# Channel shuffle on one core: the head's small tiles are merged, and the 38 KB tiles walk the array in pairs

## The chip, the core and the metric

The kernel runs on one core of a Trainium2 chip. The core has a vector engine (DVE), a scalar engine (ACT), a GpSimd engine (POOL), a sync engine (SP) and a tensor engine (PE). It has 128 partitions of on-chip memory (SBUF), and 16 DMA engines that move data between SBUF and the device memory (HBM). The time is device microseconds (us) of one execution; smaller is better.

## The reference

```python
# x: (16, 64, 64, 256) float32, groups = 8
channels_per_group = c // groups            # 32
x = x.reshape(batch, h, w, groups, channels_per_group)
x = x.transpose(0, 1, 2, 4, 3)
x = x.reshape(batch, h, w, c)
```

Each of the 65,536 pixels has 256 channels, which is 1 KB. Inside a pixel, an 8 x 32 matrix of channels is transposed to 32 x 8. No arithmetic is done and no value leaves its pixel. 67.11 MB are read and 67.11 MB are written.

## The kernel before

Input and output are seen as flat arrays of pixels. A *tile* is a stretch of pixels that is laid over the 128 partitions, q pixels to a partition; since a pixel has 1 KB, q is also the number of KB that each partition holds. The list `_SLOTS` (line 12) says how the 512 pixels of each partition are cut up:

- slot 0 has two pieces, 4 KB and 8 KB a partition, which share one input buffer and one output buffer;
- slot 1 has one piece of 28 KB;
- slots 2 to 13 have one piece of 38 KB each;
- slot 14 has one piece of 16 KB.

The loop at line 45 runs over the slots. `rows` (line 39) cuts a contiguous stretch of P * q pixels out of the flat array and gives each partition q of them in a row, so that the pixels of partition p + 1 begin where those of partition p end. A piece takes three steps:

- **Load**, line 55: `nc.sync.dma_start`, issued by SP. On the DMA side these are the packets of queue q1.
- **Copy**, line 57: `nc.vector.tensor_copy` on DVE, which reads the channels as (group, channel in group) and writes them as (channel in group, group), from the input buffer into the output buffer.
- **Store**, line 61: `nc.scalar.dma_start`, issued by ACT. These are the packets of queue q10.

Both DMAs of a piece move 128 rows, one for each partition, and a row is contiguous in HBM and in SBUF. In the trace each row is one packet: 16 loads of 128 rows are 2,048 packets, and 16 semaphore packets of 4 bytes for each load make up the other 256 of the 2,304 that the page counts for q1. A DMA engine handles 8 of the 128 rows.

There are two input buffers and three output buffers (lines 13 and 14), each as large as the biggest slot. So the load of slot n has to wait until the copies of slot n - 2 have read that input buffer, and the copies of slot n have to wait until the stores of slot n - 3 have left that output buffer. Within an engine the order is that of the program (`manual_schedule`, line 43). SP issues nothing but loads, ACT nothing but stores, DVE nothing but copies; POOL and PE take no part.

Of the kernel before, what the change touches and what calls it, by code (L numbers as in the profile page):

```python
# [1 line left out]

# [4 lines left out]


F32 = mybir.dt.float32
P = 128  # L10

_SLOTS = [[4, 8], [28]] + [[38]] * 12 + [[16]]
_IN_BUFS = 2
_OUT_BUFS = 3


@with_exitstack
def kernel(
    ctx: ExitStack,
    tc: tile.TileContext,  # L20
    x: bass.AP,
    groups: bass.AP,
    out: bass.AP,
):
    nc = tc.nc
    b, h, w, c = x.shape
    G = int(groups)
    CPG = c // G
    assert G * CPG == c
    assert sum(map(sum, _SLOTS)) * P == b * h * w  # L30
    biggest = max(map(sum, _SLOTS))

    x_flat = x.rearrange("b h w c -> (b h w c)")
    out_flat = out.rearrange("b h w c -> (b h w c)")

    in_pool = ctx.enter_context(tc.tile_pool(name="in_pool", bufs=_IN_BUFS))
    out_pool = ctx.enter_context(tc.tile_pool(name="out_pool", bufs=_OUT_BUFS))

    def rows(flat, first, q):

        return flat[first * c : (first + P * q) * c].rearrange("(p f) -> p f", p=P)

    ctx.enter_context(tc.manual_schedule(engines=None))
    first = 0
    for parts in _SLOTS:
        in_tile = in_pool.tile([P, biggest * c], F32, name="in_tile")
        out_tile = out_pool.tile([P, biggest * c], F32, name="out_tile")
        at = 0
        pieces = []
        for q in parts:  # L50
            pieces.append((q, first, slice(at * c, (at + q) * c)))
            first += P * q
            at += q
        for q, start, cols in pieces:
            nc.sync.dma_start(out=in_tile[:, cols], in_=rows(x_flat, start, q))  # L55
        for q, start, cols in pieces:
            nc.vector.tensor_copy(  # L57
                out=out_tile[:, cols].rearrange("p (i j g) -> p i j g", j=CPG, g=G),
                in_=in_tile[:, cols].rearrange("p (i g j) -> p i j g", g=G, j=CPG),
            )  # L60
            nc.scalar.dma_start(
                out=rows(out_flat, start, q), in_=out_tile[:, cols]
            )


# [1 line left out]
_INS = ['x', 'groups']  # L67
_OUTS = [((16, 64, 64, 256), 'float32')]

_NUMBERS = {'groups': 8}  # L70


# [26 lines left out]
```

## Time and profile before

| what | value |
|---|---|
| time, median of 3 runs | 316.12 us (316.09 to 316.13) |
| span of the profiled execution | 314.4 us (314.44 from the first instruction to the last) |
| DVE busy | 119.0 us in 16 copies, 38% of the span |
| one copy of a 38 KB tile | 8.79 us (mean of 12) |
| HBM | 67.11 MB read, 67.11 MB written, 427 GB/s over the span |
| load of a 38 KB tile, issue to landing | 37.0 us (median of 12) |
| store of a 38 KB tile, issue to landing | 42.6 us (median of 12) |

The time of the runs is 1.7 us more than the span: what lies outside the first and the last instruction is counted in the one and not in the other. The issue-to-landing times are longer than a transfer takes, since a DMA is issued while the one before it on its queue is still running. The share of a DMA queue on the page is the time that its packets took, as a share of 16 engines over the whole span.

### The profile page before, as it was taken

What the parts mean: (1) busy time and instruction counts of PE and PEld (TensorE: products, weight loads), DVE (VectorE), ACT (ScalarE), POOL (GpSimd) and SP (SyncE); (2) the same over time, 40 slices, a digit from 0 to 9 for tenths busy, and PEclk for the clock granted to TensorE, in tenths of its full rate; (3) what the DMA queues carried; (4) which work ended last, traced back from release to release, by engine and by line L of the source; (5) the groups of instructions that cost most, each with busy time, mean ns of one, the idle gap of its engine ahead of it and who ended that gap; (6) DMA issues with size and microseconds to landing.
All of it is one profiled execution on the core that took longest, in us unless ns stands there. A gap on an engine that the chain in (4) does not pass through costs nothing.

```text
span 314.4 us, 132 instructions
## 1 busy us (share of the span) xinstructions
DVE 119.0 (38%) x16; POOL 0.2 (0%) x4
## 2 busy tenths in 40 slices
DVE  2081907309109109019028028037046055065400
POOL 0000000000000000000000000000000000000000
DMA  7999999999999999999999999999999999999997
GB/s 317 405 441 416 435 416 483 401 465 406 450 421 446 426 436 436 401 470 396 475 396 475 396 470 401 470 401 470 401 450 421 446 426 436 436 417 450 429 421 321
DMA packets 4608, 134.22 MB, mean 427 GB/s; under 512 B 512, under 2 KB 512, under 8 KB 768
## 3 DMA queue, kind: packets, MB, share of 16 engines
q1 hardware_dynamic: 2304, 67.11, 49.8%
q10 hardware_dynamic: 2304, 67.11, 49.4%
HBM read 67.11 MB, written 67.11 MB: 427 GB/s over the span
## 4 chain that ended last, share of the span: by engine, by line
DMA 76%; DVE 19%; issue 0%; SPq 0%; DVEq 0%
DMA in_tile<-in_x_dram 76%; DVE out_tile L57 19%; SPq L55 0%; DVEq L57 0%
## 5 line engine op out<-in xcount | busy, mean ns | idle before, releaser
L57 DVE COPY out_tile<-in_tile 128x9728 f32<-128x9728 f32 (+4 forms) x16 | 119.0, 7440 | 179.4 <-DMA in_tile<-in_x_dram 179.4
L80 POOL MEMSET const-uint8-127<- 128x1 uint8 x1 | 0.1, 103 | 0.0
L80 POOL MEMSET const-bfloat16-1.0<- 128x1 bf16 x1 | 0.1, 102 | 0.0
L80 POOL MEMSET const-float32-1.0<- 128x1 f32 x1 | 0.1, 100 | 0.0
L80 POOL MEMSET const-float32-0.0<- 128x1 f32 x1 | 0.1, 99 | 0.2 <-issue 0.2
## 6 DMA issues: line engine op xcount, KB each, us to landing
in_tile<-in_x_dram SPq DMA_DIRECT2D x12, 4864.0 KB, 37.0
out_dram<-out_tile ACTq DMA_DIRECT2D x12, 4864.0 KB, 42.6
in_tile<-in_x_dram SPq DMA_DIRECT2D x1, 3584.0 KB, 14.7
out_dram<-out_tile ACTq DMA_DIRECT2D x1, 3584.0 KB, 30.9
in_tile<-in_x_dram SPq DMA_DIRECT2D x1, 2048.0 KB, 30.4
out_dram<-out_tile ACTq DMA_DIRECT2D x1, 2048.0 KB, 15.2
in_tile<-in_x_dram SPq DMA_DIRECT2D x1, 1024.0 KB, 5.4
out_dram<-out_tile ACTq DMA_DIRECT2D x1, 1024.0 KB, 25.0
```

The lines of the kernel that those rows point to most:

```text
L57: nc.vector.tensor_copy(out=out_tile[:, cols].rearrange("p (i j g) -> p i j g", j=CPG, g=G), in_=in_tile[:, cols].rearrange("p (i g j) -> ...
L80: nc = _bacc.Bacc("TRN2", target_bir_lowering=False, num_devices=1)
```

## The change

The list of slots becomes thirteen tiles of 38 KB and one of 18 KB. The pieces of 4, 8 and 28 KB at the head are gone, and so is the 16 KB piece at the end. The first 38 KB tile is taken with `rows` as before. The next twelve are taken in six pairs by a new function, `pair_half`: a pair is a contiguous stretch of 2 * P * 38 pixels in which each partition owns 76 in a row. The first tile of the pair takes the first 38 of each partition's 76, the second tile the last 38. So a row is still 38 KB and contiguous, but in HBM the rows of neighbouring partitions now begin 76 KB apart instead of 38 KB. The output is addressed in the same way. The last tile, 18 KB a partition, uses `rows`.

```diff
-_SLOTS = [[4, 8], [28]] + [[38]] * 12 + [[16]]
+_SLOTS = [[38]] * 13 + [[18]]

+    def pair_half(flat, first, q, half):
+        pair = flat[first * c : (first + 2 * P * q) * c].rearrange("(p f) -> p f", p=P)
+        return pair[:, half * q * c : (half + 1) * q * c]
...
+    paired = 0
...
         for q in parts:
-            pieces.append((q, first, slice(at * c, (at + q) * c)))
+            cols = slice(at * c, (at + q) * c)
+            if q == biggest and first:
+                half = paired % 2
+                start = first - half * P * q
+                source = pair_half(x_flat, start, q, half)
+                target = pair_half(out_flat, start, q, half)
+                paired += 1
+            else:
+                source = rows(x_flat, first, q)
+                target = rows(out_flat, first, q)
+            pieces.append((q, source, target, cols))
             first += P * q
             at += q
-        for q, start, cols in pieces:
-            nc.sync.dma_start(out=in_tile[:, cols], in_=rows(x_flat, start, q))
-        for q, start, cols in pieces:
+        for q, source, target, cols in pieces:
+            nc.sync.dma_start(out=in_tile[:, cols], in_=source)
+        for q, source, target, cols in pieces:
             nc.vector.tensor_copy(
...
-            nc.scalar.dma_start(
-                out=rows(out_flat, start, q), in_=out_tile[:, cols]
-            )
+            nc.scalar.dma_start(out=target, in_=out_tile[:, cols])
```

Buffers, engines and the order of the three steps stay: SP issues 14 loads instead of 16, DVE runs 14 copies instead of 16, ACT issues 14 stores instead of 16.

## The prediction

> **What bounds the kernel now.** I read the page's engine and DMA-queue parts first, then the chain of waits, then the table of stretches with each stretch's DMA rate.
>
> ```profile
> DVE 119.0 (38%) x16; POOL 0.2 (0%) x4
> ...
> q1 hardware_dynamic: 2304, 67.11, 49.8%
> q10 hardware_dynamic: 2304, 67.11, 49.4%
> ...
> DMA in_tile<-in_x_dram 76%; DVE out_tile L57 19%; SPq L55 0%; DVEq L57 0%
> ```
>
> DVE works 38% of the span. The two DMA queues together fill 99.2% of all 16 engines' time. The chain's 19% for DVE must not be read as "a faster copy gains 19%": the chain goes load, copy, next load into the freed buffer, and while the copy runs the engines work through the other buffer's load and the stores. That is to be seen in the second view, whose columns are the stretch, its length, DVE, POOL, clock, DMA share and GB/s:
>
> ```profile
> 1.75:9.11 7.36, 3.11 (x2) 0.00 (x0) 1.00 1.00 400
> 9.11:34.60 25.49, 10.99 (x2) 0.00 (x0) 1.00 1.00 420
> 34.60:117.35 82.75, 30.73 (x4) 0.00 (x0) 1.00 1.01 436
> 117.35:278.19 160.84, 61.61 (x7) 0.00 (x0) 1.00 1.00 434
> ...
> 294.54:313.28 18.74, 3.87 (x1) 0.00 (x0) 1.00 0.95 411
> 313.28:314.44 1.16, 0.00 (x0) 0.00 (x0) 1.00 0.00 0
> ```
>
> I cut it where the records of DMA packets change character. At 1.75 us the first packet starts, at 9.11 the first store packet, at 34.60 the first packet of the 28 KB store; from 294.54 only stores are left, and 313.28 is the end of the last packet. From 34.60 on the rate is flat at 434 to 436 GB/s. Only the head (400, then 420) and the very end (411) are below. So the bound is the rate of the DMA engines, and everything the change can win or lose without disturbing that rate lies in the first 35 us.
>
> What sets 434? In the packet records a 4 KB row takes 159 ns and a 38 KB row (38,912 bytes) 1,439 ns, in nearly all of the 3,072 cases. The slope is (1439 - 159) / (38912 - 4096) = 0.0368 ns a byte, that is 27.2 GB/s an engine, and about 8 ns a row do not depend on size. Seven tile periods of the steady part (the copies that start at 117.35 and 278.19) last 160.84 us, 22.98 each, or 1,436 ns for each of an engine's 16 rows. Bytes alone are 38912 x 0.03676 = 1,430.6 ns, so a row costs 5.5 ns beside its bytes (successive packets overlap by 3 ns in the records). That is all there is to save in the steady part: 0.4%.
>
> **The change part by part.** The reckoning is done for one engine, which moves 8.39 MB in both directions together: 8388608 x 0.03676 ns = 308.4 us. Before, it has 16 x 8 x 2 = 256 rows; 256 x 5.5 ns = 1.4; together 309.8. The trace has 313.28 - 1.75 = 311.5 from the first packet to the last, so 1.7 us are lost. The packet records say where, as a mean over the engines:
>
> - 0.22 us: the engines start their first row up to 0.56 us apart;
> - 0.29: the 4 KB load's rows take longer than 159 ns, nearly all of it the first row of each engine;
> - 0.05 and 0.26: the rows of the 8 KB and 28 KB loads (32 ns, 3%, on each 28 KB row);
> - 0.18: the first 38 KB load, at 16 to 29 us (22 ns, 1.5%, a row);
> - 0.36: one single row of the second 38 KB load, at 32.9 us, which takes about 1.81 us instead of 1.44 on all 16 engines at once;
> - the rest, some 0.3, is that the engines do not all end together.
>
> The first five, the single row included, sum to 1.36. The table of stretches gives the same: (1 - 400/434) x 7.36 + (1 - 420/434) x 25.49 = 0.57 + 0.82 = 1.39. All these slow rows are loads in a stretch where loads run almost alone; in the steady part, where loads and stores alternate, load rows of the same size are not slow, nor are the store rows at the end.
>
> *Two loads, two copies and two stores fewer.* 32 rows an engine go, 32 x 5.5 ns = -0.18 us. The page shows 5.4 us from issue to landing for the 8 KB load and 3.3 for the 4 KB load, but the later ones queue behind the earlier ones, and the engines' records have no gap between them: rows of the 8 KB load start at 3.43 us, before the last row of the 4 KB load has ended at 3.67. The copies on DVE become 13 x 8.79 + 3.87 x 18/16 = 118.6 us against 119.0, worth nothing, because each lies beside a load and a store. The issues on SP and ACT (0.33 and 0.36 us each) lie beside transfers too. [...]
>
> *The first stores are issued later.* Before, the first store is issued at 5.19 us. Now the first load must land whole: 1.75 + 0.2 + 0.3 + 8 x 1.46 = 13.9, plus 0.5 from the last packet's end to DVE's start (0.33 to 0.68 for the four loads at the head), plus the copy's 8.79: 23.2 us, at which the first store and the third load are issued. The engines are not idle meanwhile, for the second load is queued behind the first. It lasts until 13.9 + 11.7 = 25.6. What changes is that rows 2 to 16 of every engine are loads running alone. At 22 ns a row (the first 38 KB load) that is 0.33 us, at 3% of 1,439 (the 28 KB row) 0.65; I take 0.5. First-row delay and stagger, 0.29 + 0.22, stay. The single slow row of 0.36 may have belonged to the old handover from small stores to large ones, or not: bounds 0 and 0.36, value 0.18. The head's loss is then 0.22 + 0.29 + 0.5 + 0.18 = 1.19 against 1.36: -0.17. Bounds: 0.84 to 1.52, that is -0.52 to +0.16.
>
> *The cover of the first copy.* From the first load's landing the second gives the engines 11.7 us of work. Waiting, copy and the way from issue to the first packet (0.73 to 1.75, thus 1.02) take 0.5 + 8.79 + 1.02 = 10.3. 1.4 us are left, so I price it at nothing; beyond 1.4 every microsecond costs one. Behind the third load, SP has only loads that need the next copies, so it delays nothing else.
>
> *The pairs.* Rows stay 38 KB, 8 to an engine, and the packet count is the same. Only the distance between rows in HBM doubles, to 76 KB. The trace has distances of 4, 8, 16, 28 and 38 KB, none with gaps between rows. For stores all five cost the same 0.0368 ns a byte beside their 8 ns; for loads that alternate with stores so does 38. On the gain side nothing can come in the steady part beyond 5.5 ns a row (13 x 16 = 208 such rows an engine, 1.1 us), and a row still needs its packet. On the loss side the nearest row is the 3% of loads running alone: on the second tile alone, 0.35 us more. I take 0, since neither distance nor size has moved a row's time so far. [...]
>
> *The end.* The last load brings 18 KB instead of 16, and its copy takes 4.36 us instead of 3.87. Covered: after the last load lands, 18.7 us of stores are still to go. Last packet to end of span stays 1.16 us.
>
> Sum: -0.18 - 0.17 = -0.35 us on a span of 314.44: 314.1. The runs' median lies 1.68 above the span, so 315.8 us (-0.11%).
>
> **The rivals.** I count 0.2%, about what a measurement of this kernel can tell from no change, as the border: 315.49 to 316.75 is no change.
>
> *Faster.* The single slow row goes (-0.36), lone loads lose only 22 ns a row (0.33, against the 0.49 that the old 8, 28 and first 38 KB loads lost: -0.16) and 32 rows fewer give -0.18: 316.12 - 0.70 = 315.4. For it: the slow row came just before a new store's first packet. Against it: the 28 KB rows lost 3%, which is the purer case of lone loads. If the pairs help the second load too, 315.1. 24%.
>
> *Slower by a gap at the head.* The old first store was issued at 5.19 us, yet its first packet started at 9.12, 3.9 us later. If the third load needs as long as this one instead of 1.02, the cover of 1.4 is gone: 3.9 - 1.02 - 1.4 = 1.5 us idle, and 315.8 + 1.5 = 317.3. It decides from 1.0 us idle. Against it: those 3.9 us were spent behind load rows in flight, with the engines busy. 14%.
>
> *Slower by the distance of 76 KB.* Each 1% on the rows of twelve tiles is 12 x 0.23 = 2.8 us, so 1% gives 318.6; it decides from 0.4% (6 ns a row). Against it: between stores, load rows show no loss at all. 10%.
>
> *No effect of the pairing at all* is part of the forecast.
>
> **How the numbers follow.** The forecast, no change, has 52%, its own range 315.5 to 316.5. The time is its 315.8. The range 315.1 to 317.3 takes in the faster case and the head's gap, and leaves out the distance case and a few per cent of extremes. Faster 0.24, same 0.52, slower 0.14 + 0.10 = 0.24.
>
> **What would show it.** Right: 14 copies; first store issued near 23 us; no stretch of the head in which the 16 engines stand idle between 23 and 28 us; 434 GB/s in the steady part and 22.98 us from one copy to the next; q1's share still a little above q10's; q10 silent until about 25 us and stores alone for some 20 us at the end. Wrong: a tile period above 23.1 us (the distance), a hole near 26 us (the cover), or a head whose lone loads run below 420 GB/s.

## The result and the profile after

The changed kernel takes 330.74 us (median of 4 runs, 330.02 to 332.63) against 316.12: 1.047 times as long, 95% interval 1.0426 to 1.0514. The forecast was no change, at 315.8 us. The profiled execution is the run of 332.63 us, with a span of 330.9 against 314.4: 16.5 us more.

The DMA queues of the page after (packets, MB, share of 16 engines' span):

```profile
q10 hardware_dynamic: 2016, 67.11, 50.5%
q1 hardware_dynamic: 2016, 67.11, 47.6%
```

The order of the two lines has turned round. Before, the stores (q10) took 49.4% of 314.4 = 155.3 us of each engine, now 50.5% of 330.9 = 167.1: 11.8 us more for the same bytes. The loads (q1) went from 156.6 to 157.5. The stores have become slow, not the loads.

The table of stretches after, with the same columns as before:

```profile
1.74:25.30 23.56, 8.86 (x1) 0.00 (x0) 1.00 1.00 420
25.30:29.00 3.70, 2.37 (x1) 0.00 (x0) 1.00 1.02 263
...
52.77:272.09 219.32, 79.52 (x9) 0.00 (x0) 1.00 1.00 413
...
324.00:329.53 5.53, 0.00 (x0) 0.00 (x0) 1.00 0.43 183
```

Three things are to be seen. From 25.3 to 29.0 us the rate falls to 263 GB/s: a hole where the third load begins, (1 - 263/434) x 3.7 = 1.5 us. In the long middle the rate is 413 instead of 434 although the engines are busy all the time (DMA share 1.00). At the end most engines have nothing left to do (share 0.43).

The copies show the same middle as a longer period (timeline after):

```profile
15.12 8.86 DVE L72 COPY out_tile<-in_tile 128x9728 f32<-128x9728 f32 x1 [15.12 <-DMA in_tile<-in_x_dram]
24.01 11.85 ACTq L76 DMA_DIRECT2D out_dram<-out_tile  x2
26.63 8.84 DVE L72 COPY out_tile<-in_tile 128x9728 f32<-128x9728 f32 x1 [2.65 <-DMA in_tile<-in_x_dram]
52.77 8.85 DVE L72 COPY out_tile<-in_tile 128x9728 f32<-128x9728 f32 x1 [17.30 <-DMA in_tile<-in_x_dram]
...
272.09 8.84 DVE L72 COPY out_tile<-in_tile 128x9728 f32<-128x9728 f32 x1 [15.27 <-DMA in_tile<-in_x_dram]
```

From 52.77 to 272.09 lie nine periods of 24.37 us, 1.39 us more for each tile than the 22.98 of the kernel before, whose seven periods lie between these two copies (timeline before):

```profile
117.35 8.76 DVE L57 COPY out_tile<-in_tile 128x9728 f32<-128x9728 f32 x1 [14.25 <-DMA in_tile<-in_x_dram]
278.19 8.73 DVE L57 COPY out_tile<-in_tile 128x9728 f32<-128x9728 f32 x1 [14.21 <-DMA in_tile<-in_x_dram]
```

The packet records say which packets these are. A 38 KB load row still takes 1,439 ns. A 38 KB store row takes 1,583 ns in the middle (mean from 52.77 to 272.09 us), 10% more, and 1,439 again at the end, once the last loads have landed. Over an engine's 13 x 8 store rows that is 11.9 us. The rest: the loads' slow first rows cost 2.4 us where the slow rows before had cost 1.1, and the engines idle for 3.8 us on average instead of 0.6. Of these 3.2 us more, 2.6 are at the end, where one engine finishes at 329.5 us and the others between 324 and 327. 11.9 + 1.3 + 3.2 = 16.4 of the 16.5 us.

So two questions stood: which part of the change makes store rows slow, the distance of 76 KB or the new head; and by what.

### The profile page after: what moved, and what is told of

Read it like the earlier page. It is cut to its first block, busy times and chain, and to the rows that moved or that the text cites. A ratio compares the mean times of both kernels' runs of the same rounds, so it can differ in the third digit from the quotient of the medians.

```text
span 330.9 us, 121 instructions
## 1 busy us (share of the span) xinstructions
DVE 119.4 (36%) x14; POOL 0.2 (0%) x4
## 3 DMA queue, kind: packets, MB, share of 16 engines
q10 hardware_dynamic: 2016, 67.11, 50.5%
## 4 chain that ended last, share of the span: by engine, by line
DMA 78%; DVE 17%; issue 0%; SPq 0%; DVEq 0%
DMA in_tile<-in_x_dram 78%; DVE out_tile L72 17%; SPq L70 0%; DVEq L72 0%
## 5 line engine op out<-in xcount | busy, mean ns | idle before, releaser
L72 DVE COPY out_tile<-in_tile 128x9728 f32<-128x9728 f32 (+1 forms) x14 | 119.4, 8528 | 198.0 <-DMA in_tile<-in_x_dram 198.0
```

Of the source, the lines that this page charges most:

```text
L72: nc.vector.tensor_copy(out=out_tile[:, cols].rearrange("p (i j g) -> p i j g", j=CPG, g=G), in_=in_tile[:, cols].rearrange("p (i g j) -> ...
```

## The experiments

### Which part: the head or the pairs

Four kernels, each with one part.

```diff
 # head_only: after, without the pairs
-                source = pair_half(x_flat, start, q, half)
-                target = pair_half(out_flat, start, q, half)
+                source = rows(x_flat, first, q)
+                target = rows(out_flat, first, q)
 # pairs_old_head: after, with the old list of tiles
-_SLOTS = [[38]] * 13 + [[18]]
+_SLOTS = [[4, 8], [28]] + [[38]] * 12 + [[16]]
 # pair_loads: as pairs_old_head, stores contiguous
+                target = rows(out_flat, first, q)
 # pair_stores: as pairs_old_head, loads contiguous
+                source = rows(x_flat, first, q)
```

> Only the new list of tiles, thirteen of 38 KB and one of 18 KB, all with contiguous rows 38 KB apart; no pairs. Theory D (distance: rows 76 KB apart make store rows slow beside loads): the store rows go back to 1,439 ns, the tile period to 22.98 us, and only the gap near 26 us that the changed kernel shows (about 2 us) is left: 317 to 319 us. Theory H (head: the new head sets the engines in step in another way, and that makes the store rows slow): store rows stay near 1,583 ns, period near 24.3, about 330 us.

> The old list of tiles (4, 8, 28 KB, twelve of 38, 16 KB), with the twelve 38 KB tiles in pairs for loads and stores. Theory D: store rows near 1,580 ns while loads run beside them, period near 24.3 us, 326 to 331 us in all. Theory H: as before the change, 316 us, period 22.98.

> The old list of tiles; the loads of the twelve 38 KB tiles go in pairs (rows 76 KB apart), the stores keep rows 38 KB apart, so the output's pixels stand in another order; same bytes. Theory D, if what counts is where the stores write: 316 us, store rows 1,439 ns. If what counts is how load rows and store rows lie to each other, or where the loads read: between 320 and 330 us. Theory H: 316 us.

> The old list of tiles; the stores of the twelve 38 KB tiles go in pairs (rows 76 KB apart), the loads keep rows 38 KB apart, so the output's pixels stand in another order; same bytes. Theory D, if what counts is where the stores write: 326 to 331 us, store rows near 1,580 ns. If the loads' distance is needed too, less or nothing: 316 to 322 us. Theory H: 316 us.

| kernel | median us | ratio to before, 95% |
|---|---|---|
| head_only | 331.29 | 1.048 (1.044 to 1.053) |
| pairs_old_head | 316.21 | 0.999 (0.997 to 1.002) |
| pair_loads | 316.18 | 1.000 (0.999 to 1.001) |
| pair_stores | 316.15 | 1.000 (0.999 to 1.001) |

The queue lines of head_only's page are those of the changed kernel to 0.1%:

```profile
q10 hardware_dynamic: 2016, 67.11, 50.6%
q1 hardware_dynamic: 2016, 67.11, 47.6%
```

Theory D has fallen: pairs_old_head should have been slow, and pair_stores too if the stores' distance alone mattered. The distance of 76 KB cost nothing here, on either side (316.15 to 316.21 us). All of the loss comes from the list of tiles.

### How the head does it: the lead of the loads over the stores

Packet records carry no engine number, but in the steady part a packet starts within 4 ns of the end of the one before it, so most engines can be followed through. Nearly all 16 engines move in step: a round of load rows, a round of store rows, and so on. In the kernel before, all 16 end their rows of a load within about 0.5 us, in the changed kernel 14 of them within about 0.8. Number the load rows of an engine through from the first 38 KB tile (8 a tile) and the store rows in the same way, and call the difference between a store row and the load row just ahead of it the *lead*. In the kernel before it is 18 for six rows and 17 for two rows of each tile. In the changed kernel and in head_only it is exactly 16, two tiles, on nearly all engines that could be followed: the third load and the first store are issued together at 24.0 us, the moment the first copy is done. The second load is then nearly through (its last rows end between 25.4 and 26.3 us) and no store is ahead, so the two start almost level, load row first. The store row behind load row r of one tile is then row r of the tile two before. The two queues also change transfers at the same moment.

Two kernels move the lead by a hair and little else. The extra row or rows go into a buffer that nobody reads.

```diff
 # nudge_new: head_only, plus
+        if slot == 0:
+            extra = extra_pool.tile([P, 1 * c], F32, name="extra")
+            nc.scalar.dma_start(out=extra[:32, :], in_=rows(x_flat, 0, 1)[:32, :])
 # nudge_old: before, plus
+        if slot == 4:
+            extra = extra_pool.tile([P, 1 * c], F32, name="extra")
+            nc.sync.dma_start(out=extra[:16, :], in_=rows(x_flat, 0, 1)[:16, :])
```

> The new list of tiles with contiguous rows, and between the first and the second store ACT issues one extra load of 32 rows of 1 KB into a buffer that nothing reads: two short rows for each engine, 0.1 us of packets, which let the loads get ahead of the stores by two or three rows more. In the slow kernel's records the loads stand exactly 16 rows (two tiles) ahead of the stores on an engine, and store rows take 1,580 ns; in the kernel before they stand 17 and 18 rows ahead, and store rows take 1,439. Theory O (order: the exact 16 is what makes the store rows slow): store rows 1,439 ns, period 22.98, 317 to 320 us with the gap at 26 us still there. Theory G (the gap near 26 us and the 3 us first rows after it throw the engines out of step, and that makes them slow): the gap is not touched, so 330 us.

> The kernel before, and behind the third 38 KB load SP issues one extra load of 16 rows of 1 KB into a buffer that nothing reads: one short row for each engine, so that the loads lose one row, or two with the change of transfers, of their lead over the stores. No gap at the head. Theory O: where the lead becomes 16 rows, store rows become slow, and the time goes to between 318 and 328 us; if the lead goes to another number than 16 it tells nothing. Theory G: 316.3 us.

Both came out as theory O has it: at a lead of 16 the store rows became slow (1,611 and 1,589 ns in nudge_old from the third on), at leads of 17 to 19 they did not (1,439). nudge_new, with 32 KB more to move than head_only, takes 319.92 us instead of 331.29 (1.012 times before, 1.009 to 1.016). nudge_old, with 16 KB more than the kernel before and its head untouched, takes 326.49 instead of 316.15 (1.033, 1.031 to 1.034). Here are nudge_old's rounds from the packet records; each line is one round of 16 engines, and the extra row is not counted in the lead:

```
start us  queue  row of tile   mean ns   lead
   66.17  store  tile 3 row 4     1439     18
   67.60  load   tile 5 row 7     1439
   69.04  store  tile 3 row 5     1439     18
   70.48  store  tile 3 row 6     1439     17
   71.91  load   the extra row      46
   71.96  store  tile 3 row 7     1439     17
   73.40  load   tile 6 row 0     1439
   74.84  store  tile 4 row 0     1439     16
   76.27  load   tile 6 row 1     1439
   77.71  store  tile 4 row 1     1489     16
   79.17  load   tile 6 row 2     1439
   80.60  store  tile 4 row 2     1611     16
   82.28  load   tile 6 row 3     1439
   83.71  store  tile 4 row 3     1589     16
```

Until 71.9 us this is the kernel before. One short row takes a place on the load queue, the lead becomes 16, and within three rows the stores are slow. They stay so until the loads run out. nudge_old's timeline shows the period change with it:

```profile
49.01 8.92 DVE L58 COPY out_tile<-in_tile 128x9728 f32<-128x9728 f32 x1 [10.17 <-DMA in_tile<-in_x_dram]
71.19 8.81 DVE L58 COPY out_tile<-in_tile 128x9728 f32<-128x9728 f32 x1 [13.26 <-DMA in_tile<-in_x_dram]
98.28 8.72 DVE L58 COPY out_tile<-in_tile 128x9728 f32<-128x9728 f32 x1 [18.28 <-DMA in_tile<-in_x_dram]
122.39 8.80 DVE L58 COPY out_tile<-in_tile 128x9728 f32<-128x9728 f32 x1 [15.38 <-DMA in_tile<-in_x_dram]
146.60 8.88 DVE L58 COPY out_tile<-in_tile 128x9728 f32<-128x9728 f32 x1 [15.41 <-DMA in_tile<-in_x_dram]
```

The distances between the last three starts, 24.1 and 24.2 us, are those of the slow kernels; the wait ahead of each of these copies is 15.4 us instead of the 14.2 of the kernel before. So theory G is out as the cause of the slow stores: nudge_old has no hole at the head and is slow, nudge_new keeps the hole and is fast in the middle. nudge_new's stretches:

```profile
25.00:29.00 4.00, 2.41 (x1) 0.00 (x0) 1.00 1.03 282
50.00:280.00 230.00, 90.20 (x11) 0.00 (x0) 1.00 1.00 432
```

In its first tile of stores, from 28 to 57 us, nudge_new still stands at a lead of 16: those eight rows go from 1,439 to over 1,570 ns. From the second tile on the lead is 18 to 19 and a store row takes 1,439. What it keeps is the price of the hole, with the head's slow rows, the slow first tile of stores (0.9 us) and the engines ending less together: 319.92 - 316.15 = 3.8 us.

Two more kernels ask for the cause in other ways.

```diff
 # shift_stores: head_only, with stores further on in HBM
-                target = rows(out_flat, first, q)
+                target = rows(out_flat, first + 37, q if q == biggest else q - 1)
 # three_in: head_only
-_IN_BUFS = 2
-_OUT_BUFS = 3
+_IN_BUFS = 3
+_OUT_BUFS = 2
```

> The new list of tiles with contiguous rows, and all stores write 37 pixels (37 KB) further on in the output; the last store has one pixel a partition less, so 128 pixels are not written. On-chip buffers, rows, queues and order stay. Theory A (addresses: store rows are slow because load and store rows at the same time lie exactly two tiles and a constant apart in HBM): 316 to 320 us. If it is the order on the queues or the on-chip side: store rows stay near 1,580 ns, 330 us.

> The new list of tiles with contiguous rows, three input buffers and two output buffers instead of two and three: the third load is issued at the start, so there is no gap near 26 us. Theory G: store rows 1,439 ns, period 22.98, 315.5 to 316.5 us. Theory O: it depends on the lead that comes out; at 17 or more rows the same time as by theory G, at 16 near 328 us.

shift_stores takes 330.84 us (1.046, 1.044 to 1.047), and its stores still take 50.7% of the span (head_only 50.6%): the exact distance in HBM between stores and loads is not the cause, for 37 KB more left the stores as slow. three_in was meant to close the hole and ran into another bound, 348.37 us (1.101, 1.097 to 1.104). Its waits say which:

```profile
DVE out_tile L72 <- DMA out_dram<-out_tile: 196.7, 12, 19.9
```

Twelve of its 14 copies wait for a store to leave one of only two output buffers, 16 us each on average, and the engines idle for 24 us on average. Neither theory had this in view, and the time decides nothing between them.

Its packet records do say something of the lead. From about 200 to 276 us the lead is 24, three tiles, on most engines, and each tile begins after a break. Here are the store rows that followed the load row of the same number without a gap, mean of 36 or 37 tiles of an engine:

```
row of tile       0     1     2     3     4     5     6     7
mean ns        1439  1439  1440  1452  1504  1557  1568  1455
```

So 16 is not the only slow lead. At three tiles the slowness comes back, after some four to five rows, and the break before the next tile takes it away again; row 7, with that break behind it, is already nearly free of it.

### Why a lead of 16: the same partitions, or both queues changing at once

At a lead of 16 two things coincide. An engine's store row reads the same partition that the load row ahead of it wrote, in another buffer; and both queues change transfers together. (The records carry no partition number: that row r of a load and row r of a store belong to the same partition is inferred from the two transfers having the same shape.) To part them, transfers were cut into two of 64 partitions, with the stores' two in the same order as the loads' or in the other.

```diff
 # halves_same, halves_swapped: head_only, plus
+            for lo in (0, 64):
+                nc.sync.dma_start(
+                    out=in_tile[lo : lo + 64, cols], in_=source[lo : lo + 64, :]
+                )
...
+            for lo in (0, 64):          # halves_swapped: (64, 0)
+                nc.scalar.dma_start(
+                    out=target[lo : lo + 64, :], in_=out_tile[lo : lo + 64, cols]
+                )
 # evens_same, evens_swapped: the same with lo in (0, 1) and slices lo::2;
 # the stores of evens_swapped take (1, 0)
```

> The new list of tiles with contiguous rows, every load and every store cut into two transfers of 64 partitions, the first half (partitions 0 to 63) before the second on both queues. Four rows an engine and transfer instead of eight. If the lead comes out as 16 rows again, an engine's load row and the store row behind it have the same place in their tiles and the same partitions. Theory P (same partitions: an engine that writes and reads the same partitions in turn is slow) and theory C (coincidence: the two queues change transfers at the same moment) both: store rows slow, 325 to 335 us.

> As the kernel with halves in the same order, but the stores take partitions 64 to 127 first. At a lead of 16 rows the queues still change transfers at the same moment, while an engine's load row and store row now belong to partitions 64 apart. Theory P: store rows back to 1,439 ns, 317 to 321 us. Theory C: as slow as the kernel with the same order.

Neither could tell: 430.32 us (1.359 times before) and 437.16 (1.377). The loads are at half rate from the start, alone, before any store runs. The first 25 us of halves_same:

```profile
0.00:25.00 25.00, 0.00 (x0) 0.20 (x4) 1.00 0.96 199
```

199 GB/s at a DMA share of 0.96; a lone 38 KB load row takes 3.0 us. The next pair avoids that by taking even and odd partitions. In the same stretch evens_same moves 397 GB/s, as head_only does with 398:

```profile
0.00:25.00 25.00, 8.77 (x1) 0.20 (x4) 1.00 0.95 397
```

> The new list of tiles with contiguous rows, every load and store cut into two transfers of 64 partitions, even ones first, then odd ones, on both queues. If lone loads run at full rate (rows of 1,440 to 1,500 ns in the first 25 us) the run can tell: theory P (the same partitions written and read in turn) and theory C (both queues change transfers at the same moment) both expect store rows near 1,580 ns at a lead of 16 rows, 325 to 335 us. If lone load rows take 2,000 ns or more, it tells nothing.

> As the kernel with even partitions first on both queues, but the stores take the odd partitions first. Theory P: store rows 1,439 ns at a lead of 16 rows, 317 to 321 us. Theory C: as slow as with the same order, 325 to 335 us. If lone load rows take 2,000 ns or more, it tells nothing.

evens_same takes 332.83 us (1.051, 1.042 to 1.059), evens_swapped 319.34 (1.009, 1.007 to 1.011). Followed through the records, the engines of both stand at a lead of 16 rows, one engine of evens_swapped at 17, and the queues change transfers together. The DMA queues from 100 to 280 us, evens_same:

```profile
DMA packets 2357, 74.05 MB, mean 411 GB/s; under 512 B 454, under 2 KB 454, under 8 KB 454
...
q10 hardware_dynamic: 1186, 37.32, 53.0%
q1 hardware_dynamic: 1171, 36.73, 47.2%
```

and evens_swapped:

```profile
DMA packets 2483, 77.90 MB, mean 433 GB/s; under 512 B 481, under 2 KB 481, under 8 KB 481
...
q10 hardware_dynamic: 1243, 39.03, 50.2%
q1 hardware_dynamic: 1240, 38.87, 50.0%
```

37.32 MB are 959 rows of 38,912 bytes; 53.0% of 16 x 180 us over 959 is 1.59 us a store row, against 1.44 a load row (47.2%, 944 rows). With the stores' order turned round, the same sum gives 1.44 for both. Lead, sizes, number of transfers and their coinciding changes are the same in the two kernels; what differs is whether the store row that follows a load row on an engine reads the partition just written or its neighbour. (Its place in HBM differs by one row too, 38 KB; in shift_stores 37 KB there changed nothing, 330.84 us against 331.29.) Theory P (the same partition) stands, theory C (the two queues changing at the same moment) has fallen.

### Milder heads

```diff
 # split_first: head_only
-_SLOTS = [[38]] * 13 + [[18]]
+_SLOTS = [[19, 19]] + [[38]] * 12 + [[18]]
 # one_small: before
-_SLOTS = [[4, 8], [28]] + [[38]] * 12 + [[16]]
+_SLOTS = [[12], [28]] + [[38]] * 12 + [[16]]
```

> The new list of tiles with contiguous rows, but the first tile in two pieces of 19 KB in one buffer, as the old list had 4 and 8 KB: the first copy and store come at about 8 and 13 us, the buffer is free at about 19 us instead of 24, and the second load still has some 6 us to run then. Theory O: no gap, a lead of 17 rows or more, 315.7 to 316.7 us. If the lead is 16 all the same, 326 us or more with no gap at the head.

> The kernel before, with the pieces of 4 and 8 KB at the head made into one of 12 KB: one load, copy and store less, 16 rows an engine less at 5.5 ns, the next load issued at about the same time (8.7 us). Theory O: the lead stays 17 and 18 rows, 316.0 us, no change that can be told. If the lead comes out as 16 instead: 326 us.

split_first takes 318.01 us (1.007, 1.004 to 1.009), one_small 318.70 (1.006, 1.004 to 1.009). Both had been expected near 316 us. In both the store rows take 1,439 ns, as theory O has it, at leads of mostly 18 to 20 in split_first and of 13 to 15 in one_small, where 17 and 18 had been expected. one_small's long middle is at the full rate:

```profile
50.00:280.00 230.00, 87.86 (x10) 0.00 (x0) 1.00 1.00 433
```

What they lose, they lose at the head and in that the engines end less together: in the last microseconds the engines idle for 1.0 us on average in split_first and 2.1 in one_small, against 0.3 in the kernel before, and one_small's last engine ends at 315.7 us while the first have ended near 313. Small effects of the head on the engines' stagger cost up to 2.5 us here; what sets the stagger was not tried. No kernel of these beats the one before.

## Why the prediction was wrong, point by point

**The bound.** Right: the kernel is bound by the DMA engines' rate, before and after; DMA share 1.00 throughout the middle. Wrong was what I took from it: "everything the change can win or lose without disturbing that rate lies in the first 35 us". I treated the 434 GB/s as a constant of the rows' size, on the ground that 1,439 ns stood in nearly all of 3,072 rows. In the steady part all those rows had been moved at leads of 17 and 18. In these runs the rate went with the order in which loads and stores met on an engine (434 GB/s at leads of 17 and 18, 413 at 16), and the head fixed that order for the whole run.

**"The first stores are issued later".** This is the step that failed. I priced it by lone loads at the head (-0.17 us). Its effect lies 30 to 300 us further on: the third load and the first store now start level, at a lead of 16, and 11.9 us are lost on store rows. That "what is moved" may be a phase and not only an amount of work was not in my list.

**The cover of the first copy.** Priced at nothing with 1.4 us to spare; it did not hold. First load row of the third tile: issued at 24.0 us, begun between 25.5 and 27.3 on the various engines, and some 3 us long on most. The rival of the gap named the right place: the load began 1.5 to 3.3 us after its issue, not 1.02 as I had taken, though not 3.9 either. (The first store's first row did begin 3.87 us after its issue, at 27.88.) The rival's 1.5 us idle did not come in that form. The engines stood idle for 0.5 us on average, and the first rows of the third load took 1.5 us more than 1,439 ns. With all that goes with it the hole is worth some 3 us: 3.2 by evens_swapped, and 2.9 by nudge_new (3.8 less the 0.9 of its slow first tile of stores). That gives about 319, not 331.

**Lone loads.** Sized at 0.5 us, 22 to 43 ns a row. The second tile's rows, all lone, took 1,439 to 1,444 ns: nothing. Only the first row of each engine was slow (0.73 us on average).

**32 rows fewer, -0.18 us.** Too small to be told in these runs.

**The pairs.** Priced at 0: right, 316.15 to 316.21 us in three kernels. The rival of the distance (10%) was wrong, and my chance for a slower kernel (24%) lay partly on it.

**The largest slow result had no case of its own.** Each rival kept the middle of the run as it was or changed it by an address. None asked what else repeats once for every row.

## What to carry to other kernels

When loads and stores share the same DMA engines for a whole run, look at the order of their rows in the records before a head is redrawn, not only at the rate: here a lead of a whole number of tiles (16 and 24 rows were seen) put a store row behind a load row of the same partition, as inferred above, and at 16 it cost 10% of each store row (1,583 ns against 1,439). One short row an engine was enough to enter that state (nudge_old, 326.49 us) and two to leave it (nudge_new, 319.92), so in a kernel with such a lead a deliberate offset is worth a trial, such as short extra rows or the stores' partitions taken in another order: the first brought the slow list of tiles from 331.29 us to 319.92 here, the second from 332.83, with its transfers cut in two, to 319.34. And a part that looks suspicious by its addresses should be run alone first: here that cleared it at once (316.15 to 316.21 us).

## What the runs showed of the hardware that was not expected

- Store rows of 38 KB that followed, on the same DMA engine, load rows of the same partition (as inferred from the shapes) took 1,583 ns on average in the changed kernel, 1,611 and 1,589 in nudge_old and 1.59 us in evens_same instead of 1,439, although the two lay in different buffers and different HBM tensors. The slowness set in only after several such rows in a row: the third one had it in nudge_old (1439, 1489, 1611 ns), the fifth to seventh in three_in (1504, 1557, 1568 ns), where each break between tiles took it away again. With the neighbouring partition instead, evens_swapped was free of it (1.44 us). What inside the chip does this is open.
- In the changed kernel the state was one of single engines, not of all at once. The engine that ended its third load first stood at a lead of 17 for seven of its eight rows, and its store rows took 1,439 ns in both tiles through which it was followed, against the mean of 1,583. The first load ends of each tile stay 22.98 to 23.2 us apart until 212 us, and the first engine comes to be up to 12 us ahead of the last.
- Loads cut into partitions 0 to 63 and 64 to 127 moved 199 GB/s in the first 25 us (halves_same), loads cut into the even and the odd partitions 397 (evens_same). What makes the difference was not shown.
- The first store, issued while loads were still running, had its first row only 3.9 us after the issue in the kernel before, the changed one and split_first (9.12 - 5.19, 27.88 - 24.01, 22.19 - 18.25), and 4.3 us in one_small (14.53 - 10.26).
